# RMS norms between sub-layers in pairs of channel blocks, their weights multiplied in place by ScalarE

## The chip, the cores and the metric

The kernel runs on one core of a Trainium2 chip. The metric is the device time of one execution in microseconds. The core's engines each run their own queue in order: TensorE (PE in the rows, PEld its weight loads), VectorE (DVE), ScalarE (ACT), GpSimd (POOL) and SyncE (SP, which issues most DMAs).

## What is computed

One inference step of two layers for 520 tokens (512 of a prompt, 8 of a sample group), width 1024. Layer 0 is a mixer (Mamba heads and sparse attention), layer 1 a conformer convolution, and each is followed by a ConvFFN. Each of these four sub-layers is wrapped in two norms:

```
def rms_norm(x, g):
    y = x * rsqrt(mean(x * x, axis=-1) + EPS)
    return y * g
...
hp = hp + rms_norm(f(rms_norm(hp, g[0])), g[1])
```

The conformer has a layer norm of its own inside, with mean and variance over the same 1024 channels.

## The kernel before

Activations lie with channels on the partitions: 1024 channels are 8 blocks (KD) of 128, and the 520 tokens are columns, worked on in two halves of 256 and 264 (HALF). All matmuls are in three parts: a value is split into a high part rounded to fp32r (xh, wh, gh) and the rest (xl, wl, gl), and `mm3` (L312 to L314) sums wh·xh, wh·xl and wl·xh.

The sub-layers follow as mixer, boundary a, ConvFFN 0, boundary b, conformer, boundary c, ConvFFN 1, boundary d. A boundary, made by `boundary` and called once for each half, is the postnorm of what stands behind and (but for d, which stores the output) the prenorm of what comes:

- `sumsq` (L321 to L333): for each of 8 blocks ScalarE squares it (tile sq, L327), VectorE adds the squares of a group of blocks (L329), and TensorE sums a group over channels by a matmul with ones into one PSUM tile (ns, L333). How many blocks make a group stands in SQP, SQR, SQL, SQE and SUMB.
- `rstd`: Ln (L348) and Exp (L349) on ScalarE make 1/sqrt of the mean. Both functions need an activation table that gelu and sigmoid don't share, so `table` (L339) preloads it behind the last square; where the scheduler puts a gelu between, the compiler adds loads that bear the line of the function.
- `postnorm`: for each block VectorE makes xf = f·g·r (L385, in one of two buffers of a temporary tile, XFB) and adds it to the residual h (L387). f is facc, the sub-layer's output.
- `prenorm`: ScalarE makes xh = h·g (L366), VectorE xl = h·g - xh (L367); the sum of squares of h gives rsx, which is multiplied in only after the next sub-layer's first matmul (L446 in the ConvFFN, L582 in the conformer).

In the ConvFFN, `pair` computes a gate and a value block: matmuls into PSUM (up, two buffers), times rsx (L446), the convolution's taps (c: L448 on ScalarE, L451 on VectorE), gelu (ge, L459), their product gm (L461), and its two parts gh (L463, ScalarE) and gl (L464, GpSimd). `down` multiplies groups of pairs with the down weights into PSUM (dn, two buffers) and VectorE adds the result to facc (L478). The last pairs are done half by half (weights named ue), and then the last group's down products of that half with the boundary behind them. In the conformer, `gated` makes pw, multiplies by rsx (L582) and applies a sigmoid (L586); `norm` (L651, L656) is its layer norm and works in pairs of blocks.

The program's order is not written out by hand: a tile scheduler with a simulated timeline decides where each instruction stands in its engine's queue, within what tiles, buffers and data allow. On the chip each queue runs in that order.

## Time and profile before

| | us |
|---|---|
| median of 3 runs | 1960.81 (1960.59 to 1962.98) |
| the profiled execution | 1961.67 |
| its span | 1959.9 |
| TensorE busy | 1835.2 (94%) |
| VectorE busy | 1415.3 (72%) |
| ScalarE busy | 974.4 (50%) |

The span is divided, in time, into the mixer (to about 890 us), ConvFFN 0 (to about 1300), the conformer (to about 1530) and ConvFFN 1. Busy time is what the engine's instructions take in all; the rows of a timeline give an instruction's start and length, and in brackets how long its engine had been idle and whose instruction let it go on. In this trace one matmul of L333 appears as two records (x2).

### The profile page before, as it was taken

What the parts mean: (1) busy time and instruction counts of PE and PEld (TensorE: products, weight loads), DVE (VectorE), ACT (ScalarE), POOL (GpSimd) and SP (SyncE); (2) the same over time, 40 slices, a digit from 0 to 9 for tenths busy, and PEclk for the clock granted to TensorE, in tenths of its full rate; (3) what the DMA queues carried; (4) which work ended last, traced back from release to release, by engine and by line L of the source; (5) the groups of instructions that cost most, each with busy time, mean ns of one, the idle gap of its engine ahead of it and who ended that gap; (6) DMA issues with size and microseconds to landing.
All of it is one profiled execution on the core that took longest, in us unless ns stands there. A gap on an engine that the chain in (4) does not pass through costs nothing.

```text
span 1959.9 us, 38005 instructions
## 1 busy us (share of the span) xinstructions
PE 1835.2 (94%) x14449; PEld 1706.1 (87%) x14449; DVE 1415.3 (72%) x3385; ACT 974.4 (50%) x2093; POOL 189.5 (10%) x226
## 2 busy tenths in 40 slices
...
GB/s 296 114 140 197 76 190 130 149 138 129 126 90 57 92 243 136 157 143 100 87 143 165 132 105 109 87 81 53 119 107 119 87 87 116 122 119 120 148 62 49
DMA packets 125947, 240.90 MB, mean 123 GB/s; under 512 B 16499, under 2 KB 63236, under 8 KB 125444
## 3 DMA queue, kind: packets, MB, share of 16 engines
...
## 4 chain that ended last, share of the span: by engine, by line
PE 43%; DVE 5%; ACT 3%; DMA 2%; issue 1%; SPq 0%; POOL 0%; DVEq 0%; ACTq 0%; POOLq 0%
PE up L312 8%; PE up L313 8%; PE up L314 8%; PE dn L312 4%; PE dn L313 4%; PE dn L314 4%; PE dn L624 2%; PE pw L312 1%; PE pw L313 1%; PE pw L314 1%; PE ns L333 1%; DMA raw_dn<-in_w_down 1%; DVE xf L385 1%; DVE h L387 1%; DVE facc L631 1%
## 5 line engine op out<-in xcount | busy, mean ns | idle before, releaser
L312 PE MATMUL dn<-gh,wh_dn 128*128 128x256 f32 (+1 forms) x704 | 198.0, 285 | 4.8 <-ACT gh L463 2.6
L314 PE MATMUL dn<-gh,wl_dn 128*128 128x256 f32 (+1 forms) x704 | 198.9, 284 | 0.0
L313 PE MATMUL dn<-gl,wh_dn 128*128 128x256 f32 (+1 forms) x704 | 198.4, 283 | 0.0
L451 DVE SCALAR_TENSOR_TENSOR c<-up,vec,c 128x511 f32<-128x511 f32 (+2 forms) x216 | 138.9, 645 | 16.1 <-ACT c L448 15.7
L312 PEld LDWEIGHTS dn<-gh,wh_dn 128*128 128x128 f32 x704 | 131.5, 189 | 6.8 <-DVE facc L478 3.7
L313 PEld LDWEIGHTS dn<-gl,wh_dn 128*128 128x128 f32 x704 | 133.1, 189 | 0.1
L314 PEld LDWEIGHTS dn<-gh,wl_dn 128*128 128x128 f32 x704 | 132.8, 189 | 0.0
L464 POOL TENSOR_TENSOR gl<-gm,gh 128x520 fp32r<-128x520 f32 (+2 forms) x54 | 61.8, 1145 | 700.6 <-ACT gh L463 700.5
L446 DVE TENSOR_TENSOR up<-up,rsx 128x520 f32<-128x520 f32 (+2 forms) x108 | 65.0, 603 | 81.5 <-PE up L314 79.9
L478 DVE TENSOR_TENSOR facc<-dn,facc 128x256 f32<-128x256 f32 (+1 forms) x160 | 66.2, 423 | 66.4 <-PE dn L314 66.1
L293 ACT ACTIVATE wh_up<-raw_up 128x1024 fp32r<-128x1024 f32 x68 | 72.0, 1058 | 71.8 <-PE up L313 46.5
L312 PE MATMUL acc<-x0hm,wh_xz 128*128 128x256 f32 x320 | 96.3, 301 | 6.9 <-ACT u L1001 4.5
L294 DVE TENSOR_TENSOR wl_up<-raw_up,wh_up 128x1024 fp32r<-128x1024 f32 x68 | 83.1, 1222 | 23.0 <-ACT wh_up L293 22.9
L314 PE MATMUL acc<-x0hm,wl_xz 128*128 128x256 f32 x320 | 94.3, 295 | 0.0
L313 PE MATMUL acc<-x0lm,wh_xz 128*128 128x256 f32 x320 | 94.1, 294 | 0.0
L313 PE MATMUL acc<-x1lm,wh_xz 128*128 128x264 f32 x320 | 92.8, 290 | 0.0
L312 PE MATMUL acc<-x1hm,wh_xz 128*128 128x264 f32 x320 | 92.6, 289 | 0.0
L448 ACT ACTIVATE c<-up,vec 128x520 f32<-128x520 f32 (+2 forms) x108 | 74.9, 695 | 34.8 <-DVE up L446 34.4
L314 PE MATMUL acc<-x1hm,wl_xz 128*128 128x264 f32 x320 | 92.1, 288 | 0.0
L293 ACT ACTIVATE wh_dn<-raw_dn 128x1024 fp32r<-128x1024 f32 (+1 forms) x48 | 47.4, 988 | 87.7 <-PE dn L313 62.8
L294 DVE TENSOR_TENSOR ptl<-pT,pth 128x512 fp32r<-128x512 f32 (+1 forms) x96 | 65.0, 684 | 25.8 <-ACT pth L293 25.6
L293 ACT ACTIVATE pth<-pT 128x512 fp32r<-128x512 f32 (+1 forms) x96 | 56.3, 595 | 53.1 <-PE pT L1186 49.9
...
## 6 DMA issues: line engine op xcount, KB each, us to landing
...
```

Source lines behind the costliest of these rows:

```text
L293: nc.scalar.activation(hi, src, AF.Copy)
L294: (eng or nc.vector).tensor_sub(lo, src, hi.bitcast(F32))
L312: nc.tensor.matmul(ps, hi[:, wc], xh, start=first, stop=False)
L313: nc.tensor.matmul(ps, hi[:, wc], xl, start=False, stop=False)
L314: nc.tensor.matmul(ps, lo[:, wc], xh, start=False, stop=last)
L333: nc.tensor.matmul(ps, ones, acc[:, :n], start=i < group, stop=i == len(ks) - 1)
L446: nc.vector.tensor_mul(u(a, e0), u(a, e0), rv[:, a:e0])
L448: nc.scalar.activation(c[:, rs], u(r0, r1), AF.Identity, bias=V("fb", l * 44 + mt), scale=W(2, mt))
L451: nc.vector.scalar_tensor_tensor(c[:, a:e], u(a - d, e - d), W(2 - d, mt), c[:, a:e], op0=ALU.mult, op1=ALU.add)
L464: nc.gpsimd.tensor_sub(gl[:, rs], gm[:, rs], gh[:, rs].bitcast(F32))
L478: nc.vector.tensor_add(f, ps, f)
L624: nc.tensor.matmul(ps[i * 32:i * 32 + 32], cw[m][:, 4 * q + i], x4[m][:, i, cs], start=q == 0, stop=q == NQ[m] - 1)
```

## The change

The temporary xf goes. ScalarE multiplies facc by the norm's weight in place, block by block (L398 of the changed kernel), behind the squares; VectorE then multiplies two blocks at once by r, in place (L403), and adds two blocks at once to h (L404). `sumsq2` takes the place of `sumsq` at the boundaries and in the conformer's layer norm: ScalarE squares two blocks in one instruction (L341), the sums over a group are of pairs (L343), and each group ends in two matmuls (L348), one for each block of the pair. The group sizes, now counted in pairs, are halved, so a group holds as many blocks as before; SUMB stays at one, which is now a pair. The squares of pairs have a pool of their own (bq), and the mixer's temporaries sq and xf move to a pool (bm) that ends with the mixer.

```diff
--- before.py
+++ after.py
@@ -34,15 +34,15 @@
 NEG = -1e30
 XZ0 = 10
 SK = (8, 2)
-SQE = 2
+SQE = 1
 YB = 2
 DCB = 3
 HOLD = 6
 ACT_NORM = (0, 2)
 NQ = (5, 4, 4, 4, 4, 6, 7, 7)
-SQP = 4
-SQR = 8
-SQL = (1, 4)
+SQP = 2
+SQR = 4
+SQL = (1, 2)
 SUMB = (1, 1)
 CORDER = ("g00 g10 g20 g30 g01 g11 s02 s12 g21 s22 c02 g31 s32 c12 g42 c22 s42 g52 c32 s52 g60 s60 c42 g70 s70 c50 c60 "
           "c70 n00 g61 s61 g71 s71 c51 c61 c71 n11")
@@ -323,7 +323,7 @@
         n = ps.shape[-1]
         ks = list(ks)
         for i, k in enumerate(ks):
-            sq = wk.tile([128, 266], F32, tag="sq", name="sq", bufs=SQB)
+            sq = P["bm"].tile([128, 266], F32, tag="sq", name="sq", bufs=SQB)
             last = nc.scalar.activation(sq[:, :n], src(k), AF.Square)
             if i % group:
                 nc.vector.tensor_add(acc[:, :n], acc[:, :n], sq[:, :n])
@@ -331,6 +331,21 @@
                 acc = sq
             if i % group == group - 1 or i == len(ks) - 1:
                 nc.tensor.matmul(ps, ones, acc[:, :n], start=i < group, stop=i == len(ks) - 1)
+        return last
+
+    def sumsq2(ps, src, group):
+
+        n = ps.shape[-1]
+        for i in range(KD // 2):
+            sq = P["bq"].tile([128, 2, 266], F32, tag="sq", name="sq", bufs=3)[:, :, :n]
+            last = nc.scalar.activation(sq, src(2 * i), AF.Square)
+            if i % group:
+                nc.vector.tensor_add(acc, acc, sq)
+            else:
+                acc = sq
+            if i % group == group - 1 or i == KD // 2 - 1:
+                for j in range(2):
+                    nc.tensor.matmul(ps, ones, acc[:, j], start=i < group and j == 0, stop=i == KD // 2 - 1 and j == 1)
         return last
 
     def table(last):
@@ -363,29 +378,31 @@
         def g(k):
             return V("ng", (l * 4 + i) * 8 + k)
         for k in range(KD):
-            nc.scalar.activation(xh[:, k], src(k), AF.Copy, scale=g(k))
-            done_["pre%d" % hf] = nc.vector.scalar_tensor_tensor(xl[:, k], src(k), g(k), xh[:, k].bitcast(F32),
+            nc.scalar.activation(xh[:, k], src(k)[:, 0], AF.Copy, scale=g(k))
+            done_["pre%d" % hf] = nc.vector.scalar_tensor_tensor(xl[:, k], src(k)[:, 0], g(k), xh[:, k].bitcast(F32),
                                                                  op0=ALU.mult, op1=ALU.subtract)
         o = HALF[hf][0] - c0
         ps = psp(c1 - c0 - o)
-        last = sumsq(wk, ps, lambda k: src(k)[:, o:], range(KD), group)
+        last = sumsq2(ps, lambda k: src(k)[:, :, o:], group)
         rstd(wk, ps, 1.0 / D, "rs1", last if hf else None, rs[:, c0 + o:c1])
 
     def hrows(hf):
-        return lambda k: h[:, k, X0[hf]:HALF[hf][1]]
+
+        return lambda k: h[:, k:min(k + 2, KD), X0[hf]:HALF[hf][1]]
 
     def postnorm(wk, psp, hf, f, l, i, group=SQP, done=lambda k: None):
         c0, c1 = HALF[hf]
         ps = psp(c1 - c0)
-        last = sumsq(wk, ps, lambda k: f[:, k], range(KD), group)
+        last = sumsq2(ps, lambda k: f[:, k:k + 2], group)
+        for k in range(KD):
+            nc.scalar.activation(f[:, k], f[:, k], AF.Copy, scale=V("ng", (l * 4 + i) * 8 + k))
         r = rstd(wk, ps, 1.0 / D, "rs2", last if hf == 0 else None)
         done_["post%d" % hf] = done_["exp"]
-        for k in range(KD):
-            t = wk.tile([128, 266], F32, tag="xf", name="xf", bufs=XFB)
-            nc.vector.scalar_tensor_tensor(t[:, :c1 - c0], f[:, k], V("ng", (l * 4 + i) * 8 + k), r,
-                                           op0=ALU.mult, op1=ALU.mult)
-            nc.vector.tensor_add(h[:, k, c0:c1], h[:, k, c0:c1], t[:, :c1 - c0])
-            done(k)
+        for k in range(0, KD, 2):
+            f2, h2 = f[:, k:k + 2], h[:, k:k + 2, c0:c1]
+            nc.vector.tensor_mul(f2, f2, r[:, None].to_broadcast([128, 2, c1 - c0]))
+            nc.vector.tensor_add(h2, h2, f2)
+            done(k + 1)
 
     def new_x(name, hf):
         n = HALF[hf][1] - X0[hf]
@@ -650,7 +667,7 @@
                 for k in range(0, KD, 2):
                     nc.vector.tensor_add(c[:, k:k + 2], c[:, k:k + 2], nmu[:, None].to_broadcast([128, 2, n]))
                 ps = ns(n)
-                last = sumsq(bk, ps, lambda k: c[:, k], range(KD), SQL[hf])
+                last = sumsq2(ps, lambda k: c[:, k:k + 2], SQL[hf])
                 r = rstd(bk, ps, 1.0 / D, "rsl", last)
                 for k in range(0, KD, 2):
                     nc.vector.tensor_mul(c[:, k:k + 2], c[:, k:k + 2], r[:, None].to_broadcast([128, 2, n]))
@@ -774,7 +791,7 @@
             o, e = c0 - X0[hf], c1 - X0[hf]
             xh, xl = x_in[hf]
             for k in range(KD):
-                sq = P["bk"].tile([128, 266], F32, tag="sq", name="sq", bufs=SQB)[:, :c1 - c0]
+                sq = P["bm"].tile([128, 266], F32, tag="sq", name="sq", bufs=SQB)[:, :c1 - c0]
                 last = nc.scalar.activation(sq, x[hf][:, k, o:e], AF.Square)
                 if hf == 0 and k == 0:
                     behind_x(0, last.ins)
@@ -797,7 +814,7 @@
             c0, c1 = X0[hf], HALF[hf][1]
             xh, xl = x_in[hf]
             for k in range(KD):
-                xf = P["bk"].tile([128, 266], F32, tag="xf", name="xf", bufs=XFB)[:, :c1 - c0]
+                xf = P["bm"].tile([128, 266], F32, tag="xf", name="xf", bufs=XFB)[:, :c1 - c0]
                 with tc.issue_after(done[0].ins):
                     nc.vector.tensor_add(xf, xh[:, k].bitcast(F32), xl[:, k].bitcast(F32))
                 nc.vector.tensor_mul(xf, xf, rsm[:, c0:c1])
@@ -1605,7 +1622,7 @@
     def nsa_sample_out(gen, tp, first, PT, pnT, vcS, vnew, gather, d_yn):
 
         ys = first.tile([128, KD, NB], F32, name="ysS", bufs=1)
-        oT = P["bk"].tile([128, 266], F32, tag="xf", name="oT", bufs=XFB)[:, 0:128].rearrange("p (b h) -> p b h", b=NB)
+        oT = P["bm"].tile([128, 266], F32, tag="xf", name="oT", bufs=XFB)[:, 0:128].rearrange("p (b h) -> p b h", b=NB)
         os = tp.tile([128, 2, 128], F32, name="osS", bufs=1)
 
         def step(u):
@@ -1658,12 +1675,13 @@
             nc.sync.dma_start(h[:, :, c0:c1], I["x"][:, :, c0:c1])
         P["fp"] = ctx.enter_context(tc.tile_pool(name="fp", bufs=1, space=PSUM))
         P["wm"] = P.get("wu")
+        P["bq"] = ctx.enter_context(tc.tile_pool(name="bq", bufs=1))
         P["wu"] = ctx.enter_context(tc.tile_pool(name="wuf", bufs=4))
         P["wd"] = ctx.enter_context(tc.tile_pool(name="wdf", bufs=WDF))
         x, rs, after = boundary("a", 0, 1, 0, 2)
         return after
 
-    with tc.tile_pool(name="wum", bufs=3, side="right") as P["wu"]:
+    with tc.tile_pool(name="wum", bufs=3, side="right") as P["wu"], tc.tile_pool(name="bm", bufs=1, side="right") as P["bm"]:
         new = mixer(begin)()
     x2, rs2, after = boundary("b", 0, 3, 1, 0, sums=SUMB)
     with tc.tile_pool(name="su", bufs=1) as P["su"]:
```

Matmuls with ones outside the mixer's head are 70 instead of 47, activation table loads 33 instead of 27. The queues of GpSimd and SyncE and the order of the mixer are as before; at the boundaries the order is another. Where lines of the changed kernel stand for lines of before: L463 is L446, L465 is L448, L468 is L451, L476 is L459, L478 is L461, L480 is L463, L495 is L478, L381 and L382 are L366 and L367, L363 and L364 are L348 and L349, L354 is L339.

VectorE at boundary b, first half, from the first product with r on. Before:

```order
L385 SCALAR_TENSOR_TENSOR xf<-facc,vec,rs_16101 128x256 x2
L461 TENSOR_TENSOR gm<-ge,c_16302 128x264
L387 TENSOR_TENSOR h<-h,xf 128x256 x2
L385 SCALAR_TENSOR_TENSOR xf<-facc,vec,rs_16101 128x256 x2
L367 SCALAR_TENSOR_TENSOR x0lb<-h,vec,x0hb 128x256
L387 TENSOR_TENSOR h<-h,xf 128x256 x2
L367 SCALAR_TENSOR_TENSOR x0lb<-h,vec,x0hb 128x256
L329 TENSOR_TENSOR sq<-sq 128x256
L478 TENSOR_TENSOR facc<-dn,facc 128x264
L385 SCALAR_TENSOR_TENSOR xf<-facc,vec,rs_16101 128x256 x2
L478 TENSOR_TENSOR facc<-dn,facc 128x264
```

After:

```order
L403 TENSOR_TENSOR facc<-facc,rs_16048 128x2x256 x4
L468 SCALAR_TENSOR_TENSOR c_16222<-up,vec,c_16222 128x256
L404 TENSOR_TENSOR h<-h,facc 128x2x256 x4
L478 TENSOR_TENSOR gm<-ge,c_16222 128x264
L382 SCALAR_TENSOR_TENSOR x0lb<-h,vec,x0hb 128x256 x4
L343 TENSOR_TENSOR sq<-sq 128x2x256
L382 SCALAR_TENSOR_TENSOR x0lb<-h,vec,x0hb 128x256 x2
L343 TENSOR_TENSOR sq<-sq 128x2x256
L382 SCALAR_TENSOR_TENSOR x0lb<-h,vec,x0hb 128x256 x2
L343 TENSOR_TENSOR sq<-sq 128x2x256
L495 TENSOR_TENSOR facc<-dn,facc 128x264 x2
```

The last pair's gm, which stood behind two products, stands behind four products, a tap and four adds of pairs, and the first add of the second half's down products (128x264), which stood behind two x0lb, stands behind all eight.

ScalarE at the same place, from the last square of facc on. Before:

```order
L327 ACTIVATE sq<-facc 128x256
L339 ACT_TABLE_LOAD
L293 ACTIVATE wh_pw_16615<-raw_pw_16613 128x1024
L448 ACTIVATE c_16302<-up,vec 128x264
L348 ACTIVATE lnv<-ns,epsT 128x256
L349 ACTIVATE rs_16101<-lnv 128x256
L454 ACTIVATE fstg<-up 128x10
L463 ACTIVATE gh<-gm 128x264
```

After:

```order
L341 ACTIVATE sq<-facc 128x2x256
L354 ACT_TABLE_LOAD
L471 ACTIVATE fstg<-up 128x10
L476 ACT_TABLE_LOAD
L476 ACTIVATE ge<-c_16190 128x264
L398 ACTIVATE facc<-facc,vec 128x256 x2
L293 ACTIVATE wh_pw_16511<-raw_pw_16509 128x1024
L465 ACTIVATE c_16222<-up,vec 128x264
L363 ACT_TABLE_LOAD
L363 ACTIVATE lnv<-ns,epsT 128x256
L364 ACT_TABLE_LOAD
L364 ACTIVATE rs_16048<-lnv 128x256
```

The gelu (ge) that stood ahead of the preload stands behind it, with a table load of its own, and Ln and Exp each have one too.

TensorE at the same place, around the last sum of the first half's postnorm. Before:

```order
L313 MATMUL dn<-gl,wh_dn 128x264
L333 MATMUL ns<-sq,ones 128x256
L314 MATMUL dn<-gh,wl_dn 128x264
L312 MATMUL dn<-gh,wh_dn 128x264 x2
L312 MATMUL pw_16553<-x0hb,wh_pw_16547 128x256
L312 MATMUL pw_16580<-x0hb,wh_pw_16541 128x256
L313 MATMUL dn<-gl,wh_dn 128x264
L314 MATMUL dn<-gh,wl_dn 128x264
L313 MATMUL dn<-gl,wh_dn 128x264
L314 MATMUL dn<-gh,wl_dn 128x264
```

After:

```order
L313 MATMUL dn<-gl,wh_dn 128x264
L314 MATMUL dn<-gh,wl_dn 128x264
L348 MATMUL ns<-sq,ones 128x256 x2
L312 MATMUL pw_16449<-x0hb,wh_pw_16443 128x256
L312 MATMUL pw_16476<-x0hb,wh_pw_16437 128x256
L313 MATMUL pw_16449<-x0lb,wh_pw_16443 128x256
L314 MATMUL pw_16449<-x0hb,wl_pw_16444 128x256
L312 MATMUL pw_16449<-x0hb,wh_pw_16443 128x256
```

The rest of the group's down rows stood close behind the sum, with the conformer's rows (pw) among them; now 32 rows of pw stand between.

VectorE at boundary d, around the start of the first half's products. Before:

```order
L329 TENSOR_TENSOR sq<-sq 128x256
L478 TENSOR_TENSOR facc<-dn,facc 128x264 x2
L329 TENSOR_TENSOR sq<-sq 128x264
L385 SCALAR_TENSOR_TENSOR xf<-facc,vec,rs_23290 128x256 x2
L478 TENSOR_TENSOR facc<-dn,facc 128x264
L387 TENSOR_TENSOR h<-h,xf 128x256 x2
L478 TENSOR_TENSOR facc<-dn,facc 128x264
L385 SCALAR_TENSOR_TENSOR xf<-facc,vec,rs_23290 128x256 x2
L387 TENSOR_TENSOR h<-h,xf 128x256
```

After:

```order
L463 TENSOR_TENSOR up<-up,rsx 128x266
L343 TENSOR_TENSOR sq<-sq 128x2x256
L468 SCALAR_TENSOR_TENSOR c_23248<-up,vec,c_23248 128x256
L472 TENSOR_TENSOR c_23248<-c_23248,fhp 128x8
L468 SCALAR_TENSOR_TENSOR c_23248<-up,vec,c_23248 128x256
L478 TENSOR_TENSOR gm<-ge,c_23248 128x264
L403 TENSOR_TENSOR facc<-facc,rs_23108 128x2x256 x4
L404 TENSOR_TENSOR h<-h,facc 128x2x256 x3
L495 TENSOR_TENSOR facc<-dn,facc 128x264
L404 TENSOR_TENSOR h<-h,facc 128x2x256
```

The gated multiply of the last pair (L463) stands behind the eight adds of the first half, and the adds of the second half (128x264), two of which stood ahead of the products, stand behind four products and three adds of pairs.

## Rows read from the trace of the kernel before

**Rows 1.** The page, busy time of each engine over the span.
```profile
PE 1835.2 (94%) x14449; PEld 1706.1 (87%) x14449; DVE 1415.3 (72%) x3385; ACT 974.4 (50%) x2093; POOL 189.5 (10%) x226
```

**Rows 2.** Groups by line and shape, whole run: count, busy us, mean ns, idle before.
```profile
L329 DVE TENSOR_TENSOR sq<-sq 128x256 f32<-128x256 f32 x57 | 25.3, 444 | 4.8 <-ACT sq L327 4.1
...
L385 DVE SCALAR_TENSOR_TENSOR xf<-facc,vec,rs 128x256 f32<-128x256 f32 x32 | 15.0, 494 | 0.5 <-ACT rs L349 0.3
...
L387 DVE TENSOR_TENSOR h<-h,xf 128x256 f32<-128x256 f32 x32 | 12.6, 418 | 0.0
...
L651 DVE TENSOR_TENSOR facc<-facc,nmu 128x512 f32<-128x512 f32 x4 | 2.5, 686 | 0.6 <-ACT nmu L649 0.6
...
L339 ACT ACT_TABLE_LOAD x10 | 12.8, 1283 | 0.2
...
L366 ACT ACTIVATE x0hb<-h,vec 128x256 fp32r<-128x256 f32 x8 | 4.0, 501 | 4.8 <-DVE h L387 4.8
```

**Rows 3.** Timeline, VectorE at b: start us, length us, instruction, idle before.
```profile
1302.56 0.88 DVE L385 SCALAR_TENSOR_TENSOR xf<-facc,vec,rs 128x256 f32<-128x256 f32 x2 [0.34 <-ACT rs L349]
1303.35 0.43 DVE L461 TENSOR_TENSOR gm<-ge,c 128x264 f32<-128x264 f32 x1
1303.70 0.75 DVE L387 TENSOR_TENSOR h<-h,xf 128x256 f32<-128x256 f32 x2
...
1321.14 0.43 DVE L478 TENSOR_TENSOR facc<-dn,facc 128x264 f32<-128x264 f32 x1 [0.49 <-PE dn L314]
```

**Rows 4.** Timeline, ScalarE at b.
```profile
1297.23 0.41 ACT L327 ACTIVATE sq<-facc 128x256 f32<-128x256 f32 x1
...
1302.11 0.42 ACT L349 ACTIVATE rs<-lnv 128x256 f32<-128x256 f32 x1
...
1303.81 0.42 ACT L463 ACTIVATE gh<-gm 128x264 fp32r<-128x264 f32 x1 [1.22 <-DVE gm L461]
...
1326.79 1.28 ACT L586 ACT_TABLE_LOAD   x1
1328.08 0.47 ACT L586 ACTIVATE glu<-pw,vec 128x256 f32<-128x256 f32 x1
```

**Rows 5.** Timeline, TensorE at b, its two longest gaps.
```profile
1304.29 0.81 PE L312 MATMUL dn<-gh,wh_dn 128*128 128x264 f32 x2 [2.60 <-ACT gh L463]
...
1328.61 0.58 PE L312 MATMUL pw<-x0hb,wh_pw 128*128 128x256 f32 x1 [2.81 <-ACT glu L586]
```

**Rows 6.** Windows, TensorE at b: stretch, busy us (count), granted clock, DMA.
```profile
1320.00:1322.00 2.00, 2.00 (x17) 1.00 0.72 172
...
1329.00:1331.00 2.00, 2.00 (x11) 0.50 0.00 0
```

**Rows 7.** Timeline, VectorE at a, second half.
```profile
920.83 0.90 DVE L385 SCALAR_TENSOR_TENSOR xf<-facc,vec,rs 128x264 f32<-128x264 f32 x2 [1.20 <-ACT rs L349]
...
943.40 0.44 DVE L446 TENSOR_TENSOR up<-up,rsx 128x266 f32<-128x266 f32 x1 [1.25 <-ACT rsx L349]
```

**Rows 8.** Timeline, VectorE at c, second half.
```profile
1580.12 0.44 DVE L446 TENSOR_TENSOR up<-up,rsx 128x266 f32<-128x266 f32 x1
```

**Rows 9.** Timeline, VectorE at d, up to the program's end.
```profile
1931.40 0.44 DVE L446 TENSOR_TENSOR up<-up,rsx 128x266 f32<-128x266 f32 x1
...
1936.92 0.77 DVE L478 TENSOR_TENSOR facc<-dn,facc 128x264 f32<-128x264 f32 x2 [0.97 <-PE dn L314]
...
1947.42 0.43 DVE L478 TENSOR_TENSOR facc<-dn,facc 128x264 f32<-128x264 f32 x1
...
1950.54 0.90 DVE L385 SCALAR_TENSOR_TENSOR xf<-facc,vec,rs 128x264 f32<-128x264 f32 x2 [1.77 <-ACT rs L349]
...
1955.85 0.77 DVE L387 TENSOR_TENSOR h<-h,xf 128x264 f32<-128x264 f32 x2
```

**Rows 10.** Timeline, ScalarE at d.
```profile
1938.45 0.40 ACT L349 ACTIVATE rs<-lnv 128x256 f32<-128x256 f32 x1
```

**Rows 11.** Chain that ended last, at d: start us, length us, what.
```profile
1940.59 0.45 PE ns L333 x2
```

## The prediction

> **What bounds the kernel now.** I read the page's busy shares first [rows 1]: TensorE is busy 94% of the span and VectorE 72%, ScalarE 50%. A norm between two sub-layers is where TensorE can run dry, since its next matmuls need the normed rows. So I went on to the groups by shape for the price of each instruction that the change touches [rows 2], then to the timelines of VectorE, ScalarE and TensorE at boundary b (end of the first ConvFFN, start of the conformer) [rows 3 to 5], to the granted clock there [rows 6], and to the boundaries a, c and d [rows 7 to 11]. The reader is to see in them that at a and c the norm is VectorE's work and VectorE is late; that at b and d TensorE's queue has been laid so tightly around the norm that one late row of another engine stops it; and that after d's last sum nothing runs beside the norm, so that there every microsecond counts.
>
> The profiled execution took 1961.67 us, 0.86 above the median of 1960.81; its span is 1959.9. I sum against 1961.67 and take 0.86 off at the end.
>
> **The change, part by part.** Prices first. The durations of one xf, one h add and one pair of blocks in one instruction (L651 has that form already) are 494, 418 and 686 ns [rows 2]; but neighbours overlap in the pipeline. Two xf run 0.88 us and two h adds 0.75 [rows 3], so that each further one adds 0.39 and 0.33, and the four pairs of L651 keep VectorE busy for 2.5 us, 0.62 each [rows 2]. I reckon with 0.40, 0.34 and 0.62.
>
> *What VectorE saves.* A half's postnorm is 8 xf and 8 h adds, 8 x 0.74 = 5.9 us; after, 4 multiplies and 4 adds of pairs, 8 x 0.62 = 5.0 us. With fewer sum adds (105 of some 444 ns [rows 2] become 24 single and 29 of pairs) that is 1.5 to 2 us of VectorE per half. *What ScalarE pays.* 8 Copies with a scale; eight of that form (L366) keep it busy for 4.0 us [rows 2], so 3 to 4 us. In the order they stand between the squares, beside the sums, so little of it is on the path. *What TensorE pays.* Each group now ends in two matmuls with the ones, one for each block of the pair: 47 become 70. One costs 0.45 us on the chain (its two records are one matmul) [rows 11], so 23 cost at most 10.4 us, if all of them stood on the path; at a and c they push aside matmuls that wait anyway. *Table loads.* 27 become 33, of 1.283 us each [rows 2]; where they stand is told below.
>
> *Boundary b.* Here the order decides, and the three differences of order shown above belong together. Before, the temporary xf has two buffers, and the scheduler laid other work between the xf's: gm of the last pair stands behind the second xf, so gh came at 1303.81 and TensorE's gap was 2.60 us [rows 3 to 5]. After, without the temporary, four multiplies, a tap and four adds stand ahead of gm, and gm ahead of every x0lb. On ScalarE the preload of the Ln/Exp table is undone by a gelu load, so that Ln and Exp each bring a load of their own. The last square ended at 1297.6 and should again. From there I add the rows of ScalarE's order: four loads of 1.28, ge and Exp at 0.4, two Copies at 0.4, the next weight's cast at about 1, c and Ln at about 0.5 = 8.9, so rs stands at about 1306.5 where it stood at 1302.5 [rows 4]. VectorE then: 2.5 + 0.4 + 2.5 + 0.35, so gm ends at 1312.2 and the first x0lb at about 1312.7. TensorE's queue has 32 conformer rows right behind the sums, and the third of them reads x0lb; the rest of the second half's down projection stands behind them. So TensorE stands from about 1302.5 to 1312.5, 10 us where it was 2.6: 7.5 us more. [...] Behind it, the m2 add of the second half waits on VectorE behind two gated multiplies that need rsx, whose Ln and Exp bring two more loads; with two PSUM buffers TensorE stalls another 1.5 us. Two sums more (0.9) make **+10.5 us** at the m7 add, which was at 1321.14 [rows 3] and would be at 1331 to 1333, and at the sigmoid behind it, 1328.08 [rows 4]. Bounds: +5, if the next gap of 2.81 us [rows 5] vanishes because more conformer rows are ready by then and the extra stall doesn't come; +14, if half clock and stall come twice.
>
> [...] The rows show a table load of 1.28 us and the sigmoid 0.01 us behind it [rows 4], no more. [...]
>
> *Boundary d, the end.* In the order, the last pair's gated multiply of the second half now stands behind all eight adds of the first half, since TensorE's last up row went behind 24 down rows: 1935.0 instead of 1931.40 [rows 9]. Its c, taps and gm (0.6 + 1.0 + 0.4) follow. gh stands behind Exp in the order; rs was at 1938.45 to 1938.85 [rows 10], the two sums now cost 0.45 more, so gh is there at about 1939.5 and gl after it; TensorE reaches the rows that need gh at 1937.8 and stands 1.8 us. Then four multiplies and three adds of pairs (4.3 us) stand ahead of the first add of the second half, which was at 1936.92 and would be at 1943.7; with two PSUM buffers TensorE stands 3.0 us more. Four sums ahead of the last add cost 1.8 us. Half clock behind the stalls costs 0 to 2.6. So the m7 add moves from 1947.42 by +7 to +9. Behind it: pair square instead of square (+0.15), no sum add (-0.44), two sums instead of 0.73 (+0.2), Ln and Exp as now, and 5.0 us instead of 6.1 for the products and adds (from 1950.54 to the end of the last two h adds) [rows 9], -1.2 together; stores that come closer together could take back up to 1. **+7 us**, bounds +3 and +10.
>
> *Boundaries a and c.* VectorE is the late engine: a's second half begins its xf at 920.83 and only at 943.40 is rsx there for the next row [rows 7]; at c the row that waits for rsx in the same way comes at 1580.12 [rows 8]. After, by the same adding up along the three queues, the norm ends 2 to 3 us earlier at either, against one more table load (1.28) ahead of rsx and some six more sums, part of them in idle time. I take **-2.2 us** for a (bounds -4 and 0) and **-1.5** for c (bounds -3.5 and +1.5, where all its sums cost). *The conformer's LayerNorm*: pairs in its sums of squares, **-0.5** (bounds -1 and +1). What the mixer's temporaries do in another pool costs nothing: the order of its instructions does not change, and it needs no wait that it had not.
>
> **Sum**: +10.5 + 7 - 2.2 - 1.5 - 0.5 = +13.3 us on 1961.67 is 1975.0 in the profiled execution, 1974 as a median.
>
> **The rivals.**
>
> *Faster.* VectorE's relief at the norms counts in full. Its place is a and c, where VectorE ends the waits, and the last 6.1 us, which are VectorE's alone; it decides once the holes at b and d together are under 5 us more than now. At its best a and c give 4 and 3.5, LayerNorm 0.5, d's end 1, and b and d lose 1 instead of 17: 1961 - 8 = 1953 us. Against: a queue runs in order, and at b every x0lb stands behind eight wide instructions. [...] 0.08.
>
> *No change.* b's and d's holes come, at half their size: the gelu load is hidden while TensorE's sums are still out (rs at 1304, b +4), gh at d comes before its rows (d +3), and a, c and LayerNorm give back 4 to 6. 1961 + 1 to 3 = 1962 to 1964 us. For it: a hole at b that only delays conformer rows is partly filled by the gap of 2.81 us that follows. 0.13.
>
> *Slower, and by more.* The 23 extra sums are all on the path, since at every boundary TensorE is the engine that resumes last: then a and c lose 2 each instead of gaining, and the stores queue: +13.3 + 7.7 + 1 = 1983 us. For it: TensorE's share of 94%. Against: at a and c VectorE and ScalarE end the waits. 0.09.
>
> **How the numbers follow.** The forecast, 1966 to 1981 with 1974 as its middle, has 0.70. 0.2% (3.9 us) is about what a measurement of this kernel can tell from no change. Faster by more than that is the first rival, 0.08; within it the second, 0.13; slower the rest, 0.79. The range runs from 1960, so that it holds the second rival, to 1982, which leaves out half of the third; outside are the first rival (0.08), half of the third (0.05) and the forecast's own tails where several bounds fall together (0.06), 0.19 in all.
>
> **What would show it.** On the timeline of b: TensorE idle for 8 to 11 us with an x0lb as releaser, ahead of a conformer row; a table load ahead of both Ln and Exp; four pair multiplies and four pair adds in a block on VectorE with gm behind them. At d: the first add of the second half's down rows some 7 us later than the up multiply's shift alone explains, and TensorE idle before a down row with VectorE's facc as releaser. At a and c: rsx of the second half earlier by 1 to 3 us measured from the boundary's start. The forecast is wrong if TensorE's idle at b is under 5 us, or if the span from d's last add to the end shrinks by far more than 1 us. The step I trust least is d, where three queues run into each other within 10 us; b rests on fewer steps.

## Result and profile after

The changed kernel takes 1987.59 us (median of 4 runs, 1986.17 to 1988.92), the kernel before, run beside it, 1960.70: 1.0139 times as long, with an interval from 1.0122 to 1.0156. The profiled execution spans 1984.4 us, 24.5 more than before. The forecast was 1974, in a range from 1960 to 1982: the sign and the two places of the loss were right, the size was not.

The page of the kernel after, busy time of each engine, answers to [rows 1]:

```profile
PE 1851.3 (93%) x14495; PEld 1720.2 (87%) x14495; DVE 1397.0 (70%) x3269; ACT 1000.7 (50%) x2099; POOL 191.1 (10%) x226
```

VectorE has 18.3 us less to do and the kernel takes 24.5 us longer. TensorE is busy 16.1 us more with nearly the same matmuls (46 records more, two for each of 23 new sums).

To see where the time went, the span is cut at seven instructions that both kernels have: the first Exp of boundary a, the 9th, 52nd, 67th and 107th multiply of an up tile by rsx (of 108), and, between the 52nd and the 67th, the 9th multiply of pw by rsx. The times are read from the timelines, and the differences are after minus before:

```
                 mixer      a   ffn 0       b  conf+c   ffn 1       d
ends, before    894.16 950.80 1283.05 1353.57 1605.20 1922.32 1959.90
ends, after     892.78 948.02 1281.08 1366.26 1619.14 1937.63 1984.40
stretch longer   -1.38  -1.40   +0.81  +14.66   +1.25   +1.37   +9.19
```

"conf+c" runs from the rest of the conformer to boundary c's end, with its layer norm in it. Each stretch is read from one execution of a kernel; the medians are 26.9 us apart, so the table leaves 2.4 us out. How well a stretch repeats is shown below by two pairs of kernels with the same order of instructions: e0 against before, and e5 against after as far as d. There the mixer differs by 2.6 and 2.8 us and conf+c by 2.8 and 2.3, every other stretch by 0.7 at most. So a difference of under 3 us in the mixer or in conf+c says nothing by itself, and totals are compared by medians.

ScalarE at b, after (start us, length us, instruction, idle before), answers to [rows 4]:

```profile
1295.79 0.64 ACT L341 ACTIVATE sq<-facc 128x512 f32<-128x512 f32 x1 [1.35 <-DVE facc L495]
1296.44 1.28 ACT L354 ACT_TABLE_LOAD   x1
...
1297.92 1.28 ACT L476 ACT_TABLE_LOAD   x1
...
1301.86 1.28 ACT L363 ACT_TABLE_LOAD   x1
1303.15 0.47 ACT L363 ACTIVATE lnv<-ns,epsT 128x256 f32<-128x256 f32 x1
1303.65 1.28 ACT L364 ACT_TABLE_LOAD   x1
1304.94 0.42 ACT L364 ACTIVATE rs<-lnv 128x256 f32<-128x256 f32 x1
...
1334.24 1.28 ACT L363 ACT_TABLE_LOAD   x1
...
1336.03 1.28 ACT L364 ACT_TABLE_LOAD   x1
...
1337.76 1.28 ACT L603 ACT_TABLE_LOAD   x1
1339.06 0.47 ACT L603 ACTIVATE glu<-pw,vec 128x256 f32<-128x256 f32 x1
```

Four loads lie between the last square and rs, where one lay before, and the second half's Ln and Exp have a load each too. The sigmoid comes at 1339.06 where it came at 1328.08.

VectorE at b, after, answers to [rows 3]:

```profile
1305.39 2.50 DVE L403 TENSOR_TENSOR facc<-facc,rs 128x512 f32<-128x512 f32 x4 [2.28 <-ACT rs L364]
...
1308.20 2.49 DVE L404 TENSOR_TENSOR h<-h,facc 128x512 f32<-128x512 f32 x4
1310.60 0.43 DVE L478 TENSOR_TENSOR gm<-ge,c 128x264 f32<-128x264 f32 x1
1310.95 1.66 DVE L382 SCALAR_TENSOR_TENSOR x0lb<-h,vec,x0hb 128x256 fp32r<-128x256 f32 x4
...
1331.80 0.43 DVE L495 TENSOR_TENSOR facc<-dn,facc 128x264 f32<-128x264 f32 x1 [1.02 <-PE dn L314]
```

The block of wide work stands in front of gm and of the first x0lb. TensorE at b, after, its longest gaps (in brackets), answers to [rows 5]:

```profile
1309.48 0.79 PE L312 MATMUL pw<-x0hb,wh_pw 128*128 128x256 f32 x2 [8.89 <-ACT x0hb L381]
1311.48 0.58 PE L313 MATMUL pw<-x0lb,wh_pw 128*128 128x256 f32 x1 [1.21 <-DVE x0lb L382]
...
1339.59 0.58 PE L312 MATMUL pw<-x0hb,wh_pw 128*128 128x256 f32 x1 [5.11 <-ACT glu L603]
```

8.89 + 1.21 us stand where 2.60 stood, and 5.11 where 2.81 stood. Behind the second gap the clock is low for longer. The windows after that gap, first of the kernel before, then of after (stretch, us and busy us, count, granted clock, DMA):

```profile
1328.00:1332.00 4.00, 3.39 (x17) 0.57 0.00 0
1332.00:1336.00 4.00, 4.00 (x33) 1.00 0.00 0
```

```profile
1339.00:1343.00 4.00, 3.41 (x16) 0.50 0.00 0
1343.00:1347.00 4.00, 4.00 (x26) 0.69 0.00 0
```

In the rows of both traces the matmuls of pw start 0.21 us apart where the clock is 0.50 and 0.12 where it is 1.00; the windows at 0.57 and 0.69 hold both distances. At d, VectorE after, answers to [rows 9]:

```profile
1950.22 0.43 DVE L463 TENSOR_TENSOR up<-up,rsx 128x266 f32<-128x266 f32 x1
...
1954.49 3.05 DVE L403 TENSOR_TENSOR facc<-facc,rs 128x512 f32<-128x512 f32 x4
1957.47 1.88 DVE L404 TENSOR_TENSOR h<-h,facc 128x512 f32<-128x512 f32 x3
1959.27 0.42 DVE L495 TENSOR_TENSOR facc<-dn,facc 128x264 f32<-128x264 f32 x1
...
1972.17 0.43 DVE L495 TENSOR_TENSOR facc<-dn,facc 128x264 f32<-128x264 f32 x1 [1.02 <-PE dn L314]
```

And TensorE there, after:

```profile
1954.94 0.51 PE L312 MATMUL dn<-gh,wh_dn 128*128 128x264 f32 x2 [1.92 <-ACT gh L480]
1955.84 0.39 PE L313 MATMUL dn<-gl,wh_dn 128*128 128x264 f32 x1 [0.40 <-POOL gl L481]
...
1959.75 0.59 PE L312 MATMUL dn<-gh,wh_dn 128*128 128x264 f32 x1 [3.15 <-DVE facc L495]
```

TensorE waits first for gh, then for the first add of the second half, which stands behind the block.

At a, the second half's rsx before, and then the rows of after that answer to [rows 7] (TensorE's longest wait, for the squares that rsx is made from; ScalarE's rsx; VectorE's multiply by it):

```profile
942.94 0.42 ACT L349 ACTIVATE rsx<-lnv 128x264 f32<-128x264 f32 x1
```

```profile
928.11 2.12 PE L348 MATMUL ns<-sq,ones 128*128 128x264 f32 x4 [5.36 <-DVE sq L343]
...
934.30 0.42 ACT L364 ACTIVATE rsx<-lnv 128x264 f32<-128x264 f32 x1
...
940.73 0.44 DVE L463 TENSOR_TENSOR up<-up,rsx 128x266 f32<-128x266 f32 x1 [0.68 <-PE up L314]
```

Measured from a's start, rsx is there 7.3 us earlier, but the multiply stands only 1.3 us earlier: it now waits for TensorE. At c, ScalarE from the second half's rsx to the tap that VectorE waits for ahead of the multiply of [rows 8], before and then after:

```profile
1577.77 0.42 ACT L349 ACTIVATE rsx<-lnv 128x264 f32<-128x264 f32 x1
1578.10 0.55 ACT L448 ACTIVATE c<-up,vec 128x256 f32<-128x256 f32 x1
```

```profile
1590.04 0.43 ACT L364 ACTIVATE rsx<-lnv 128x264 f32<-128x264 f32 x1
1590.48 1.28 ACT L476 ACT_TABLE_LOAD   x1
1591.77 0.42 ACT L476 ACTIVATE ge<-c 128x256 f32<-128x256 f32 x1
1592.10 0.55 ACT L465 ACTIVATE c<-up,vec 128x256 f32<-128x256 f32 x1
```

rsx is there 0.4 us earlier, measured from the 9th pw multiply, and the tap 1.3 us later, with a load and a gelu between.

### The profile page after: what moved, and what is told of

Same layout as the page of the kernel before. It is cut to its first block, busy times and chain, and to the rows that moved or that the text cites. A ratio compares the mean times of both kernels' runs of the same rounds, so it can differ in the third digit from the quotient of the medians.

```text
span 1984.4 us, 37942 instructions
## 1 busy us (share of the span) xinstructions
PE 1851.3 (93%) x14495; PEld 1720.2 (87%) x14495; DVE 1397.0 (70%) x3269; ACT 1000.7 (50%) x2099; POOL 191.1 (10%) x226
## 4 chain that ended last, share of the span: by engine, by line
PE 45%; DVE 5%; ACT 4%; issue 1%; DMA 1%; SPq 0%; DVEq 0%; ACTq 0%
PE up L312 8%; PE up L313 8%; PE up L314 8%; PE dn L312 5%; PE dn L313 5%; PE dn L314 5%; PE dn L641 2%; PE pw L312 1%; PE pw L313 1%; PE pw L314 1%; PE ns L348 1%; DVE facc L403 1%; DVE h L404 1%; DVE facc L648 1%; DVE c L468 0%
## 5 line engine op out<-in xcount | busy, mean ns | idle before, releaser
L468 DVE SCALAR_TENSOR_TENSOR c<-up,vec,c 128x511 f32<-128x511 f32 (+2 forms) x216 | 139.0, 646 | 15.5 <-ACT c L465 15.1
L463 DVE TENSOR_TENSOR up<-up,rsx 128x520 f32<-128x520 f32 (+2 forms) x108 | 65.2, 604 | 89.5 <-PE up L314 89.1
L495 DVE TENSOR_TENSOR facc<-dn,facc 128x256 f32<-128x256 f32 (+1 forms) x160 | 66.5, 424 | 86.5 <-PE dn L314 86.0
L465 ACT ACTIVATE c<-up,vec 128x520 f32<-128x520 f32 (+2 forms) x108 | 74.8, 694 | 30.1 <-DVE up L463 29.5
```

The source lines that it names most:

```text
L463: nc.vector.tensor_mul(u(a, e0), u(a, e0), rv[:, a:e0])
L465: nc.scalar.activation(c[:, rs], u(r0, r1), AF.Identity, bias=V("fb", l * 44 + mt), scale=W(2, mt))
L468: nc.vector.scalar_tensor_tensor(c[:, a:e], u(a - d, e - d), W(2 - d, mt), c[:, a:e], op0=ALU.mult, op1=ALU.add)
L495: nc.vector.tensor_add(f, ps, f)
```

## Experiments

Each run is one kernel, and its median is compared with runs of the kernel before on the same chip (1960.4 to 1961.5). An edit is shown by its main lines, against after where nothing else is said. The stretches, longer than before by us:

```
                            mixer    a  ffn0     b  conf+c  ffn1     d
after                       -1.4  -1.4  +0.8  +14.7   +1.3  +1.4  +9.2
e0_pools_only               +2.6  +0.5  +0.7   -0.3   +2.8  +0.7  +0.0
e11_preload_behind_copies   +1.7  -1.7  +1.2   +7.8   +2.0  +1.4  +7.9
e12_preload_and_one_sum     -1.1  -0.0  +1.8   +5.3   -0.3  +1.4  +1.0
e17_products_in_turn        +2.9  -0.2  +1.5  +11.1   +4.1  +1.4  +7.8
e14_all_three_undone        -1.2  +0.7  +1.8   +0.3   +3.0  +1.6  -0.3
e5_single_sums_at_d         +1.4  -0.8  +1.1  +14.9   +3.6  +1.4  +1.0
e1_sums_in_pairs            +1.9  +7.9  -0.1  +10.9   +0.8  +0.4  +8.1
e2_products_in_place        -0.8  +0.7  -0.6   +5.6   +5.4  -0.1  +0.9
e3_products_into_temporary  -0.1  +2.9  +0.8  +11.5   +5.5  +1.4  +7.9
e4_two_square_buffers       -3.5  +1.2  +3.1  +14.0   +7.5  +1.8 +10.1
e16_in_turn_single_sums     -3.5  +1.8  -0.7   +2.3   +6.4  -0.5  -0.6
e19_no_weights_three_undone +3.4  -0.6  +1.4   -0.4   -3.7  +2.1  -0.3
e18_no_weights_in_turn      -0.0  +0.6  -0.4   +0.0   +2.1  +0.2  -0.6
```

**The pools alone.** The kernel before with the new pools: xf and the squares of the norms in bq, the mixer's in bm, all else as it was.

> The changed kernel with its arithmetic undone: single squares, sums and group sizes as before, xf in a temporary as before; only the pools stay moved (mixer temporaries in bm, squares and xf in bq). Its order on every engine equals the order before. Both theories: within 0.2% of the kernel before, 1957 to 1965 us. If it is slower by more than 3 us, the pools (addresses, releases) carry part of the loss and the reading of the order falls.

Measured: 1965.14 us, ratio 1.0017 (1.0004 to 1.0029), just above the expected 1965. The moved pools cost some 3 to 4 us (the interval allows 0.8 to 5.7) with the order unchanged, so by the sign set ahead of the run (over 3 us) the order does not explain the whole loss. None of it is at b or d; in the profile it is in the mixer and in conf+c, the two stretches that repeat least.

**The table loads at b.** The preload is issued behind the last Copy instead of the last square, so that the scheduler lays it after the gelu:

```diff
-            nc.scalar.activation(f[:, k], f[:, k], AF.Copy, scale=V("ng", (l * 4 + i) * 8 + k))
+            last = nc.scalar.activation(f[:, k], f[:, k], AF.Copy, scale=V("ng", (l * 4 + i) * 8 + k))
```

> The change, with the table's preload ahead of the postnorm's Ln placed behind the last Copy instead of the last square. TensorE's order is the changed kernel's throughout, and VectorE's but for the place of two adds at d; on ScalarE at b the gelu now stands ahead of the preload, and three pairs of loads (ahead of Ln and Exp of the first half's postnorm and prenorm and of the second half's postnorm) are gone. Theory (the loads are on the path three times): rs at b 2.5 us earlier, the second gap and the rest as much again, b's loss 15 down to 7 to 10 us, so 1980 to 1983 us. Rival (the loads are hidden behind VectorE's block, one of them at most counts): 1985 to 1989.

Measured: 1979.07 us, 1.0093 (1.0066 to 1.0120), 0.9 us under what was expected; b falls from 14.7 to 7.8, and from the last square to the sigmoid two loads are left of nine. ScalarE at b in this kernel:

```profile
1298.95 0.64 ACT L341 ACTIVATE sq<-facc 128x512 f32<-128x512 f32 x1 [1.35 <-DVE facc L495]
...
1300.78 1.28 ACT L354 ACT_TABLE_LOAD   x1
...
1303.78 0.47 ACT L363 ACTIVATE lnv<-ns,epsT 128x256 f32<-128x256 f32 x1 [0.19 <-PE ns L348]
1304.29 0.42 ACT L364 ACTIVATE rs<-lnv 128x256 f32<-128x256 f32 x1
```

From the last square's end to rs it is 4.70 us (1299.59 to 1304.29), after 8.51 (1296.43 to 1304.94): three loads fewer are 3.81 us, 1.27 each, although Ln now waits 0.19 us for the sum. The second half's Ln and Exp have no loads either, and the gap that was 5.11 is 2.81 again. Its TensorE at b:

```profile
1308.87 0.80 PE L312 MATMUL pw<-x0hb,wh_pw 128*128 128x256 f32 x2 [5.12 <-ACT x0hb L381]
1310.87 0.58 PE L313 MATMUL pw<-x0lb,wh_pw 128*128 128x256 f32 x1 [1.21 <-DVE x0lb L382]
...
1337.00 0.39 PE L312 MATMUL pw<-x0hb,wh_pw 128*128 128x256 f32 x1 [2.81 <-ACT glu L603]
```

So the loads are 6.9 us of b's 14.7. The 1.3 us that d falls by are not theirs: d has one load in both kernels, but two of VectorE's adds have another place there.

**One sum for each group.** On top of that, VectorE adds the two blocks of a group's pair at its end, and TensorE sums once:

```diff
-                for j in range(2):
-                    nc.tensor.matmul(ps, ones, acc[:, j], start=i < group and j == 0, stop=i == KD // 2 - 1 and j == 1)
+                nc.vector.tensor_add(acc[:, 0], acc[:, 0], acc[:, 1])
+                nc.tensor.matmul(ps, ones, acc[:, 0], start=i < group, stop=i == KD // 2 - 1)
```

> e11, and in addition VectorE adds the two blocks of a pair (128 columns of partitions x 256) before the sum, so that a group ends in one matmul again: 55 at the boundaries and the layer norm instead of 90, with 24 to 35 more small adds. In its order d has its last up row and its sums where the kernel before had them; b's block of wide work ahead of gm and x0lb, with 32 conformer rows behind it, is left. Theory (loads, sums' place at d, and the block are the three causes): only the block's 5 to 6 us at b is left, and a little of c: 1964 to 1970 us. Rival (what is lost at d is not the sums' doing): 1975 or more. It beats the kernel before only if a and c gain over 6 us, which no run so far shows.

Measured: 1968.90 us, 1.0041 (1.0023 to 1.0059), as expected. b falls by 2.5 more, and d from 7.9 to 1.0, more than the sums' own 0.45 us each explain: the scheduler's order at d is another with them.

**The block of wide work.** After, but each multiply by r is issued behind the add of the pair ahead of it, as two buffers of xf had enforced:

```diff
-            nc.vector.tensor_mul(f2, f2, r[:, None].to_broadcast([128, 2, c1 - c0]))
-            nc.vector.tensor_add(h2, h2, f2)
+            with tc.issue_after(ad.ins) if k else ExitStack():
+                nc.vector.tensor_mul(f2, f2, r[:, None].to_broadcast([128, 2, c1 - c0]))
+            ad = nc.vector.tensor_add(h2, h2, f2)
```

> The change, with each pair's product placed behind the add of the pair before it, so that products and adds take turns and the scheduler lays gm, x0lb and the second half's adds between them; at b the last down rows stand behind 8 conformer rows instead of 32. Table loads (36) and sums (70 at the boundaries and in the layer norm, as before this edit) stay. Theory (the block on VectorE is a cause of its own, 5 to 6 us at b): 1980 to 1984 us, TensorE's first gap at b 6 to 7.5 us instead of 8.9. Rival (with the loads in place the block is hidden behind them): 1986 to 1990.

Measured: 1986.62 us, 1.0121 (1.0093 to 1.0149). The total is in the rival's range, not the theory's. At b the first gap is 7.09 us, as the theory had it, but b is only 3.6 us shorter instead of 5 to 6; this kernel has 36 table loads, three more than after, all three in the second half's norms at b. In the profiled execution, the slowest of its four, the mixer and conf+c, the two stretches that repeat least, are longer by 4.2 and 2.8 us.

**All three undone.** e12 with that same edit, so the pairs stay, with one preload, one sum and products in turn.

> e12 (preload behind the Copies, one sum for a group) and products and adds in turn: all three causes taken out, ScalarE's weights in place and the pairs kept. Theory: b loses at most 2 us against the kernel before, d nothing, a and c within 2 us: 1961 to 1966 us, the same as before. Rival (ScalarE's Copies or the additional small adds cost by themselves): as e12, 1967 to 1971. If pairs on VectorE are worth what the durations say, it comes out under 1957.

Measured: 1967.56 us, 1.0031 (1.0019 to 1.0043). b and d are as before to 0.3 us, as the theory said; the total misses its upper end by 1.6 and is in the range of the rival, by which ScalarE's Copies or the small adds cost by themselves. conf+c is 3.0 longer, no more than in e0, which has neither. VectorE at b in this kernel:

```profile
1305.40 0.68 DVE L405 TENSOR_TENSOR h<-h,facc 128x512 f32<-128x512 f32 x1
1306.00 0.68 DVE L404 TENSOR_TENSOR facc<-facc,rs 128x512 f32<-128x512 f32 x1
1306.60 0.43 DVE L479 TENSOR_TENSOR gm<-ge,c 128x264 f32<-128x264 f32 x1
1306.94 0.48 DVE L382 SCALAR_TENSOR_TENSOR x0lb<-h,vec,x0hb 128x256 fp32r<-128x256 f32 x1
```

gm and the first x0lb stand behind two products and an add instead of eight wide instructions. Without loads and pair sums, the block is worth 5.3 - 0.3 = 5.0 us.

**Single sums at d alone.** After, but the two postnorms of d square and sum single blocks:

```diff
-        last = sumsq2(ps, lambda k: f[:, k:k + 2], group)
+        last = sumsq(P["bq"], ps, lambda k: f[:, k], range(KD), 2 * group) if single else sumsq2(ps, lambda k: f[:, k:k + 2], group)
```

> The change, but at boundary d alone squares and sums are single, in groups as before; the order of all that comes before d is the changed kernel's. Theory (at d it is the pairs of sums, by the late last up row and by gh behind Exp and by four more sums, that cost the 9 us, not VectorE's products): 1977 to 1981 us. Rival (the block of wide products and adds on VectorE makes d's loss): within 2.5 us of the changed kernel's 1987.6.

Measured: 1981.07 us, 1.0099 (1.0066 to 1.0133); d falls from 9.2 to 1.0, the rest stays. TensorE's gaps at d in this kernel:

```profile
1964.64 0.39 PE L312 MATMUL dn<-gh,wh_dn 128*128 128x264 f32 x1 [0.53 <-DVE facc L496]
1966.79 0.39 PE L312 MATMUL dn<-gh,wh_dn 128*128 128x264 f32 x1 [0.43 <-DVE facc L496]
```

The waits for gh and gl are gone, and the wait for the facc add is down to 0.53 + 0.43 us with the products still in place: adds of the second half stand ahead of the products again. So 8.2 of d's 9.2 us hang on pairs in the sums, and as e12 keeps the pairs of squares and has +1.0 too, on the second matmul of each group.

**Each part alone.** First the sums in pairs, with the postnorm of before and two buffers of squares:

```diff
-            nc.vector.tensor_mul(f2, f2, r[:, None].to_broadcast([128, 2, c1 - c0]))
-            nc.vector.tensor_add(h2, h2, f2)
+            nc.vector.scalar_tensor_tensor(t[:, :c1 - c0], f[:, k], V("ng", (l * 4 + i) * 8 + k), r,
+                                           op0=ALU.mult, op1=ALU.mult)
+            nc.vector.tensor_add(h[:, k, c0:c1], h[:, k, c0:c1], t[:, :c1 - c0])
```

> Squares and sums in pairs as in the change, postnorm as before (xf in a temporary, two buffers; squares of pairs have two buffers instead of three for want of room). In its order b's Ln and Exp bring table loads of their own (postnorm and prenorm), but the xf stay interleaved with gm, x0lb and the adds; at d the last up row went behind 24 down rows and gh behind Exp, and the sums are 70. Theory (two causes: table loads and sums from the pairs of squares, a block of wide VectorE work from the in-place products): b loses 3 to 6 us (two or three loads of 1.28 on rs, gap 6 instead of 2.6), d 3 to 6, so 1967 to 1973 us. Rival (the block on VectorE alone makes the loss): within 3 us of before. Rival (all of the loss is in the sums and loads): 1983 or more.

Measured: 1990.64 us, 1.0154 (1.0137 to 1.0171), far above the theory and in the range of the rival that gives the whole loss to sums and loads. But the two buffers, which it has for want of room, are a second change: less the 8 to 9 us that e4 gives them below it would be at about 1982, an estimate between the two. What it does tell is d: +8.1 without any block of products, where two buffers alone add 1.0 (e4 against after).

Then the products in place with single sums (sumsq for sumsq2 everywhere, group sizes of before):

```diff
-        last = sumsq2(ps, lambda k: f[:, k:k + 2], group)
+        last = sumsq(P["bq"], ps, lambda k: f[:, k], range(KD), group)
```

> Only the postnorm of the change: weights multiplied in place by ScalarE, products and adds in pairs on VectorE, no temporary; squares, sums and group sizes as before. In its order the preload of the table stays in force at b, so rs should come within 1 us of before, but four products, a tap and four adds stand ahead of gm and all x0lb, and 31 conformer rows ahead of the rest of the down rows. Theory (two causes): TensorE's gap at b is 5.5 to 7 us instead of 2.6 and the second gap 4 to 5 us instead of 2.8; d, where two adds and the up row keep their places, loses 0 to 2; a and c gain 1 to 2; sum 1966 to 1972 us. Rival (loads and sums alone make the loss): 1955 to 1961 us, the gain at a and c being all that is left.

Measured: 1974.04 us, 1.0073 (1.0056 to 1.0089), 2 us above the theory's range: d +0.9, b +5.6, in line with the block's 5.0 us, but conf+c +5.4 where a gain was expected.

**The products into a temporary** of pairs, with one buffer, and two buffers of squares for want of room:

```diff
-            nc.vector.tensor_mul(f2, f2, r[:, None].to_broadcast([128, 2, c1 - c0]))
-            nc.vector.tensor_add(h2, h2, f2)
+            t = P["bq"].tile([128, 2, 266], F32, tag="xf", name="xf", bufs=1)[:, :, :c1 - c0]
+            nc.vector.tensor_mul(t, f2, r[:, None].to_broadcast([128, 2, c1 - c0]))
+            nc.vector.tensor_add(h2, h2, t)
```

> The whole change, but each pair's product goes into a temporary of one buffer instead of in place (squares of pairs then have two buffers instead of three). In its order products, adds, gm, x0lb and the second half's adds are interleaved again at b and d; table loads, sums (70) and ScalarE's Copies are those of the change. Theory (two causes): the block's share goes, the loads' share stays: 1967 to 1975 us. Rival (ScalarE's Copies and the sums make the loss, whatever VectorE's order): within 4 us of the changed kernel, 1984 to 1991. Rival (the block alone): 1957 to 1963.

Measured: 1991.16 us, 1.0150 (1.0130 to 1.0169). Missed, and in the range of the rival that gives the loss to Copies and sums: the theory had let the loads and sums stand but gave the block some 13 to 21 us, and the two buffers add to the time. Against e4, which has two buffers too, it is 5.1 us less, 2.5 of it at b and 2.3 at d; b at +11.5 agrees with e17.

**Two buffers of squares** in after, to size that:

```diff
-            sq = P["bq"].tile([128, 2, 266], F32, tag="sq", name="sq", bufs=3)[:, :, :n]
+            sq = P["bq"].tile([128, 2, 266], F32, tag="sq", name="sq", bufs=2)[:, :, :n]
```

> The changed kernel with two buffers for the squares of pairs instead of three, and nothing else: it tells how much of what e1 and e3 lost at a and c is theirs for want of the third buffer. If the third buffer is what saved a in the changed kernel (there a and c together lost nothing, in e1 and e3 they lost 7 to 9 us), this one is at 1992 to 1998 us; if e1's and e3's losses at a and c are from xf's own order, it stays at 1984 to 1991.

Measured: 1996.30 us, 1.0186 (1.0158 to 1.0214), as expected if the third buffer is what saves a and c: it is worth 8.7 us between the medians (8.0 with each measured against its own runs of before), the scheduler's other order with it. The groups by form, ScalarE's squares of h in the first halves, of this kernel and then of after, show part of it (count, busy us, mean ns, idle before):

```profile
L341 ACT ACTIVATE sq<-h 128x512 f32<-128x512 f32 x12 | 7.5, 621 | 4.4 <-DVE sq L343 4.4
```

```profile
L341 ACT ACTIVATE sq<-h 128x512 f32<-128x512 f32 x12 | 7.4, 620 | 0.0
```

With two buffers the squares wait, 4.4 us in all, for VectorE's add of the pair before.

**Single sums, products in turn.** e2 with the preload behind the Copies and e17's edit.

> Postnorm of the change with products and adds in turn and the preload behind the Copies; squares, sums and group sizes single as in the kernel before. Theory: what e2 lost at b (5.6 us) goes, what it lost in the conformer and at c (5 us, ScalarE's Copies between the evictions there) stays in part: 1962 to 1968 us. Rival (e2's loss at c has the same cause as its loss at b): 1958 to 1962, the same as before or a little faster.

Measured: 1969.08 us, 1.0038 (1.0023 to 1.0053), 1.1 us above the expected range; b +2.3, d -0.6, but conf+c +6.4. Of all the versions that compute the norms in full, none beats the kernel before.

**ScalarE's Copies.** What was left stood in the conformer and at c, so the last two runs leave out the eight multiplies by the norm's weight:

```diff
-        for k in range(KD):
-            last = nc.scalar.activation(f[:, k], f[:, k], AF.Copy, scale=V("ng", (l * 4 + i) * 8 + k))
```

> This is e14_all_three_undone without ScalarE's eight in-place multiplies by the norm's weight at each postnorm (the weights are left out of the postnorm, so its output is another). Theory A: the gains forecast at a and c do not come because those multiplies stand on ScalarE among the next sub-layer's rows (evictions, sigmoids, weight casts), so that rows of the conformer and of boundary c come late. Then without them the stretch conformer + c, +3.0 us in e14, falls to 0 or below, b and d stay within 1 us of before, and the kernel takes 1956 to 1962 us. Theory B: it is the order of the wide work on VectorE or the sums, not the multiplies. Then conformer + c stays at +2 or more, and the kernel takes 1964 to 1968 us.

> This is e16_in_turn_single_sums without ScalarE's eight in-place multiplies by the norm's weight at each postnorm (the weights are left out of the postnorm, so its output is another). Theory A (the multiplies on ScalarE cost the conformer and boundary c): conformer + c, +6.4 us in e16, falls below +1.5, and the kernel takes 1957 to 1963 us. Theory B (order of VectorE's work): conformer + c stays at +3 or more, and the kernel takes 1965 to 1969 us.

Measured: e19 1958.93 us, 0.9994 (0.9985 to 1.0003), and e18 1961.99, 1.0005 (0.9995 to 1.0016). Against e14 and e16 that is 8.6 and 7.1 us less (7.6 and 6.0 with each measured against its own runs of before). In e19 it is where theory A put it: conf+c from +3.0 to -3.7. In e18 conf+c falls from +6.4 to +2.1, between the bounds of the two theories (+1.5 and +3), and b from +2.3 to 0.0; the total is in theory A's range. Over b, conformer and c together the two agree: 7.4 and 6.5 us less. TensorE at c, first half's last rows, e14 and then e19:

```profile
1570.80 0.55 PE L312 MATMUL up<-x0hc,wh_us 128*128 128x256 f32 x1 [7.15 <-ACT sq L341]
```

```profile
1564.51 0.55 PE L312 MATMUL up<-x0hc,wh_us 128*128 128x256 f32 x1 [2.66 <-ACT sq L341]
...
1571.58 0.36 PE L312 MATMUL up<-x0hc,wh_us 128*128 128x256 f32 x1 [1.62 <-DVE c L467]
```

These gaps, 7.15 us against 2.66 + 1.62, are 2.9 us of it. So the Copies cost some 7 us of these kernels between b and c. Leaving them out changes the scheduler's order as well, and these runs cannot split the 7 us into ScalarE's own time and the order. The number of table loads is not it (29 in e14 and e19, 29 and 28 in e16 and e18), but their place is part of it: at c, e14 and e16 have a gelu's load right behind rsx as after has, e19 and e18 have not.

## Why the prediction missed its size

The profiled pair is 24.5 us apart where +13.3 was forecast. Of the 11.2 us missing, b has 4.2, a, c and the layer norm together 4.0, d 2.2 and the stretches between them, which the sum has at nothing, 0.8.

**Boundary b: mechanism right, term too small (+10.5 predicted, +14.66 measured, above the bound of 14).** The signs set for it came, but that the long wait was released by ScalarE's x0hb and only a short one by x0lb: TensorE idle 8.89 + 1.21 us, a load ahead of Ln and of Exp, the block of eight with gm behind it. The adding up along the queues came close: TensorE's wait grew by 7.5 us, as predicted; rs stood at 1305.36 (predicted 1306.5, both ends), the m7 add, the second half's last add to facc, at 1331.80 (1331 to 1333), the sigmoid 11.0 us late (10.5). (The terms of its sum, 7.5 + 1.5 + 0.9, make 9.9 and not 10.5.) Two things made the term too small. It took its start, the last square's end, from the trace of before (1297.6; it came at 1296.43), and the stretch began 1.97 us earlier: time won ahead of b was not won in the end, and the loss within b to the sigmoid was 11.0 + 2.0 = 13.0. The sum takes a's gain off again, though this start has none of it. And it stopped at the sigmoid: its sum has no term for the clock behind the second gap. The gap there grew from 2.81 to 5.11 us, and behind it the clock stayed at 0.50 through one window of 4 us and was 0.69 in the next, where before it was 0.57 and then 1.00. In the rows of the two traces, matmuls start 0.21 us apart for 5.9 us behind that gap, where before they did for 2.9, and 0.12 apart from there on: an estimate from these distances gives 1.3 of the other 1.7 us. The experiments split the 14.7 into table loads 6.9, the block 5.0, two matmuls for one 2.5, and 0.3 that is left; taken in another order the block alone is 3.6 (e17, with three more loads), so the parts do not simply add.

The price of a table load was right: three loads fewer made ScalarE's way to rs 3.81 us shorter (e11), 1.27 each, and in the rows of after above Ln, Exp and the sigmoid start 0.01 to 0.02 us behind their loads of 1.28.

**Boundary d: direction right, size a little small (+7 predicted, +9.2 measured, within +3 to +10), one attribution wrong.** The m7 add moved from 1947.42 to 1972.17, 24.8 us, of which 15.3 us were there when the stretch began (1922.32 to 1937.63); the remaining 9.4 compare with +7 to +9. The first add of the second half came 22.4 us later (1936.92 to 1959.27): 15.3 from ahead of d, 3.5 with the up multiply, 3.5 more. The prediction's own times say 3.6 and 3.2; its sign, some 7 us beyond the up multiply's shift, does not follow from them. TensorE's waits, 1.92 and 3.15 us, were predicted at 1.8 and 3.0. The 0 to 2.6 us of half clock in the sum here, and the half clock in b's bound of +14, are prices that no run shows by themselves. What the traces show at d is a clock of 1.00 in every window of 2 us from 1931 to 1947 us before; after, behind the wait of 3.15 us, it is 0.50 from 1960 to 1962 and 0.67 in the next 2 us. Matmuls there start 0.22 us apart for 3.5 us and 0.12 apart from there on, and an estimate from these distances gives 1.6 us. From the m7 add to the end it was 12.23 us against 12.48: VectorE was done 0.8 us sooner after it (8.37 us against 9.20, its two blocks of pairs 5.04 instead of 6.08), and the way from VectorE's end to the program's, 3.28 us before and 3.86 after (stores 2.2 and 2.6 us from issue to landing, in the median), took 0.6 of that back, as the bound had allowed. But the prediction gave the second wait to the block of products, and to the sums only their own 1.8 us: that is the step that failed at d. With the block and single sums (e5) d is +1.0; without the block and with pair sums (e1) it is +8.1; with pair sums and products in turn (e17) +7.8. With the block, pairs of squares and one sum for a group (e12) it is +1.0. So two matmuls for a group, through the order that the scheduler lays around them, make 8.2 of the 9.2.

**Boundaries a, c and the layer norm: the gains of 4.2 us did not come; a gave -1.4, the conformer with c +1.25.** a's gain is 0.8 us short, and conf+c's +1.25 is less than what that stretch differs by between equal orders, so it is no more than "no gain". The step that failed is the reading that VectorE and rsx end the waits there. At a, rsx came 7.3 us earlier from the boundary's start, more than the 1 to 3 that were to show it, but the row that had waited for it came only 1.3 us earlier: it then waited for TensorE, which had stood 5.36 us for VectorE's add of squares ahead of the norm's sum. At c, the row of [rows 8] waited for rsx itself in neither kernel (rsx was there at 1578.19, the row came at 1580.12), but for ScalarE's tap behind it. A gelu with a load of its own, 1.7 us together, now stands between the two, and the row came 1.3 us later.

A second reason is ScalarE's price. Its 3 to 4 us for eight Copies were right (64 take 29.1 us in all, 3.6 for a half), but that "little of it is on the path" was read from the order and does not hold in e14 and e16. Leaving them out took 7.4 us (e14) and 6.5 us (e16) off the way from b to c, and then the kernel is as fast as before, not faster: what VectorE saves is worth about what the rest of the change still costs. What the Copies cost in the changed kernel itself, where the work is laid otherwise, no run shows.

**The small terms.** The mixer's pool was put at nothing; moving the pools alone cost 3 to 4 us (e0); its place and its mechanism are not settled. ConvFFN 0 and 1 are 0.8 and 1.4 us longer; the second is the same in after, e3, e5, e11, e12 and e17 and absent in e1, e2 and e16, and its cause stays open.

**The rivals.** "Slower, and by more" named the nearest time, 1983 us, for another reason: it put all extra sums on the path everywhere. They cost 2.5 us at b and decide d, but a and c show no clear sign of them (e12, without them, against e11: a 1.7 longer, conf+c 2.3 shorter, which is within what it differs by). "Faster" did not come: its places gave -1.4 and +1.25. "No change" had the holes at b and d at half their size; they came larger than forecast.
